# Hybrid encoder block: the low part of q in the sample's scores taken as two 64-row products, one for each half of the keys

## The chip, the cores and the metric

The kernel runs on one core of one Trainium2 chip, so no other core works beside it. The metric is the device time of one execution in microseconds (us), as the median of several runs.

## The reference

The block is computed for a prompt of 512 tokens and for a sample of 1024 tokens, with the same weights. What matters here is the attention: 4 heads, and in each head two score maps m of 64 columns each.

```
s = jnp.einsum('bqhmd,bkhmd->bhmqk', qblk, k,
               preferred_element_type=jnp.float32) * scale
s = s - slopes[None, :, None, None, None] * dist[None, None, None]
p = jax.nn.softmax(s, axis=-1)
w = p[:, :, 0] - lam * p[:, :, 1]
return jnp.einsum('bhqk,bkhd->bqhd', w.astype(v.dtype), v)
```

Ahead of it stand an RMSNorm and one projection (q, k, v and the two inputs of a recurrent branch); behind it the output projection, a residual, and a SwiGLU feed-forward part with its own norm and residual.

## The kernel before

Matrix products run on TensorE in a rounded 32-bit type (F32R). To keep the precision, a factor is split into a high part (the rounded value) and a low part (the rest), and most products are made three times: high by high, high by low, low by high. The helper `mm3` (L213, L214, L215) does that, so these three lines carry most of TensorE's work. Each matrix product is two instructions, a load of the 128x128 weights and a stream of up to 512 columns past them.

The scores have a way of their own. A map has only 64 rows to contract over, and TensorE has 128. So `both` (L493) loads each map's 64 rows of k and q twice, into rows 0 to 63 and again into rows 64 to 127. L504 rounds all 128 rows of k into the tile kt; L505 then puts the low part into rows 64 to 127. One product of 128 rows with the high part of q (tile qh, the same 64 rows twice) thus gives q-high by k-high plus q-high by k-low. A second one, with the low part of q (tile ql), is added to it in PSUM.

For the sample, each head takes 8 blocks of 128 queries (index j), and each block both maps (index m): 4 x 8 x 2 = 64 passes. A pass covers 1024 keys, in two halves of 512 that lie in two banks of PSUM (tile sc, of which there is one). It makes four products of 512 columns, two at L582 and two at L583. VectorE then reads sc with the distance table, writes pb and finds the row minimum (L585), and ScalarE takes the exponential (L588). Transposes (L534) and the products with v (tile pv) follow one block later.

All this is a generator, `attention`, whose steps are put between the steps of other work by `advance`. The sample's attention lies beside the prompt's gate and up projections (tile gu, lines L213 to L215) from about 480 to 850 us. What TensorE does in which order is fixed when the program is built: a scheduler orders the instructions of each engine, and at run time each engine goes through its own list in that order.

The lines ahead of the scores, and the loop that the change touches:

```
A.copy(K[m], r[m])
V.tensor_tensor(K[m][DK:P], r[m][DK:P], K[m][DK:P].bitcast(F32), ALU.subtract)
...
for b in range(n // BLK):
    w = slice(b * BLK, (b + 1) * BLK)
    T.matmul(sc[:, w], lhsT=qh[m][:, qs], rhs=K[m][:, w], start=True, stop=False)
    T.matmul(sc[:, w], lhsT=ql[m][:, qs], rhs=K[m][:, w], start=False, stop=True)
```

`ATT` is the number of buffers in the pool named att, from which kt, v, qh, ql, pb and the transposed weights of a head come.

Of the kernel before, what the change touches and what calls it, by code (L numbers as in the profile page):

```python
# [12 lines left out]
F32R = mybir.dt.float32r  # L13
# [7 lines left out]
P = 128  # L21
# [4 lines left out]
BLK = 512  # L26
NH = 4
DK = 64
# [12 lines left out]
NPAR = 69  # L41

N_RAW, AHEAD, LOOK, LOOK2, LOOK3, LOOK4, LATE = 3, 2, 5, 4, 4, 4, 2
M3, ATT, AL, TH, PG = 10, 15, 2, 4, 16

A1, A2, A3, A4, A5, A6, A7, A8, B1, B2, A9 = 40, 50, 0.05, 80, 180, 12, 290, 0.95, 17, 6, 120
F1, F2, F3, F4, F5, F6 = 0.3, 0.9, 0.3, 0.8, 0.3, 0.5
# [34 lines left out]
def build(tc, io, es):  # L82
    nc = tc.nc
    V, A, T = nc.vector, nc.scalar, nc.tensor
# [16 lines left out]
    def small(n, name, bufs=2):  # L101
        return smp.tile([P, n], F32, name=name, tag=name, bufs=bufs)
# [8 lines left out]
    def bank(name, tag):  # L111
        return banks[tag].tile([P, BLK], F32, name=name, tag=tag)

    def bank2(name, shape):
        return banks["sc"].tile(shape, F32, name=name, tag="sc")
# [24 lines left out]
    def split(h, l, src, eng=V):  # L140
        A.copy(h, src)  # L141
        eng.tensor_tensor(l, src, h.bitcast(F32), ALU.subtract)  # L142
# [68 lines left out]
    def mm3(out, wh, wl, ah, al, first, last, more=False):  # L211

        T.matmul(out, lhsT=wh, rhs=ah, start=first, stop=False, skip_group_check=more)  # L213
        T.matmul(out, lhsT=wh, rhs=al, start=False, stop=False, skip_group_check=more)  # L214
        T.matmul(out, lhsT=wl, rhs=ah, start=False, stop=last, skip_group_check=more)  # L215
# [260 lines left out]
    def two(n, name, dt=F32, ring="att"):  # L476

        if n == BLK:
            t = rings[ring]([P, 2, n], name, dt)
            return [t[:, 0], t[:, 1]]  # L480
        return [rings[ring]([P, n], f"{name}{m}", dt) for m in range(2)]

    def attention(s, done, vo):
        n = length[s]
        nk = n // P
        z = n / SEQ_S
        for hd in range(NH):
            while 8 + hd not in done[s]:
                yield 1.3
            tab = rings["att"]([P, TABW], "tab", F16)  # L490
            nc.sync.dma_start(tab, tabs[hd])

            def both(i, n=n, w=slice(None)):  # L493
                r = two(n, "ld", ring="main")
                for m in range(2):
                    src = qkv[s][i][m * DK:(m + 1) * DK, w]
                    nc.sync.dma_start(r[m][0:DK], src)
                    nc.sync.dma_start(r[m][DK:P], src)
                return r

            r = both(4 + hd)
            K = two(n, "kt", F32R)
            for m in range(2):
                A.copy(K[m], r[m])  # L504
                V.tensor_tensor(K[m][DK:P], r[m][DK:P], K[m][DK:P].bitcast(F32), ALU.subtract)  # L505
                yield 1.2 * z
            vr = rings[vo]([P, n], "vr")
            nc.sync.dma_start(vr, qkv[s][8 + hd])
            vh, vl = two(n, "v", F32R)
            for g in range(n // BLK):  # L510
                w = slice(g * BLK, (g + 1) * BLK)
                pt = bank("pt", "aux")
                for i in range(4):
                    T.transpose(pt[:, i * P:(i + 1) * P], vr[:, g * BLK + i * P:g * BLK + (i + 1) * P], ident)
                split(vh[:, w], vl[:, w], pt)
                yield 0.6
            ot = rings[vo]([P, n], "ot")
            z0 = small(nk, f"z0{nk}")
            ve = small(nk, f"ov{nk}")
            def weights(j, pp, zs):  # L520

                cf = small(1, "cf", 4)
                V.reciprocal(cf, zs[1])
                V.scalar_tensor_tensor(cf, zs[0], neglam, cf, ALU.mult, ALU.mult)
                V.scalar_tensor_tensor(pp[0], pp[1], cf, pp[0], ALU.mult, ALU.add)
                yield 1.5 * z
                if j % 2 == 0:
                    wt.append([[rings["att"]([P, 4, 256], f"wt{x}{i}", F32R) for i in range(nk // 4)] for x in "hl"])
                wh, wl = wt[-1]
                for i in range(nk // 4):  # L530
                    pt = bank("ptw", "aux")
                    for kk in range(4):
                        k0 = (4 * i + kk) * P
                        T.transpose(pt[:, kk * P:(kk + 1) * P], pp[0][:, k0:k0 + P], ident)  # L534
                    jq = slice(j % 2 * P, (j % 2 + 1) * P)
                    split(wh[i][:, :, jq], wl[i][:, :, jq], pt.rearrange("p (k q) -> p k q", k=4))
                    yield 0.7
                if j % 2:
                    yield from values(j // 2, wh, wl)

            def values(g, wh, wl):

                pv = bank("pv", "pv")
                for kc in range(nk):
                    w = slice(kc * P, (kc + 1) * P)
                    mm3(pv[:, 0:256], vh[:, w], vl[:, w], wh[kc // 4][:, kc % 4], wl[kc // 4][:, kc % 4],
                        kc == 0, kc == nk - 1)
                gq = slice(g * 256, (g + 1) * 256)
                A.copy(ot[:, gq], pv[:, 0:256])
                sq = rings["osq"]([P, 256], "osq")  # L550
                A.activation(sq, ot[:, gq], AF.Square)
                yield 2.0 * z

                def squares():
                    for j in range(2):
                        T.matmul(pv[:, 256 + j:257 + j], lhsT=sq[:, j * P:(j + 1) * P], rhs=ones, start=True, stop=True)

                    vg = ve[:, 2 * g:2 * g + 2]
                    zg = z0[:, 2 * g:2 * g + 2]
                    V.scalar_tensor_tensor(vg, zg, EPS, zg, ALU.mult, ALU.mult)  # L560
                    V.scalar_tensor_tensor(vg, pv[:, 256:258], 1.0 / P, vg, ALU.mult, ALU.add)

                late.append(squares)

            wt, late, prev = [], [], None
            for j in range(nk):
                if j % 4 == 0:
                    r = both(hd, BLK, slice(j * P, j * P + BLK))
                    qh, ql = two(BLK, "qh", F32R), two(BLK, "ql", F32R)
                    for m in range(2):  # L570
                        split(qh[m], ql[m], r[m])
                        yield 0.6
                q0 = j * P
                qs = slice(q0 % BLK, q0 % BLK + P)
                pp, zs = two(n, "pb"), []
                if n == BLK:
                    sc2 = bank2("sc2", [P, 2, n])
                for m in range(2):
                    sc = sc2[:, m] if n == BLK else bank2("sc", [P, n])
                    for b in range(n // BLK):  # L580
                        w = slice(b * BLK, (b + 1) * BLK)
                        T.matmul(sc[:, w], lhsT=qh[m][:, qs], rhs=K[m][:, w], start=True, stop=False)  # L582
                        T.matmul(sc[:, w], lhsT=ql[m][:, qs], rhs=K[m][:, w], start=False, stop=True)  # L583
                    mn = small(1, "mn", 4)
                    V.tensor_tensor_reduce(out=pp[m], in0=sc, in1=tab[:, 896 - q0:896 - q0 + n], scale=-0.125,  # L585
                                           scalar=3e38, op0=ALU.add, op1=ALU.min, accum_out=mn)
                    zz = z0[:, j:j + 1] if m == 0 else small(1, "z1", 4)
                    A.activation(pp[m], pp[m], AF.Exp, scale=-1.0, bias=mn, accum_out=zz)  # L588
                    zs.append(zz)
                    if late:  # L590
                        late.pop()()
                    yield 1.5 * z
                    if prev and m == SKEW[0]:
                        yield next(prev)
                    if prev and m == SKEW[1]:
                        yield from prev
                        prev = None
                prev = weights(j, pp, zs)
            yield from prev
            yield YV  # L600
            late.pop()()
            r = rsqrt_cols(ve, nk, "a")
            yield YV * z
            for g in range(n // BLK):
                w = slice(g * BLK, (g + 1) * BLK)
                bc = bcast_cols("pv", r, 4 * g, "a")
                V.scalar_tensor_tensor(ot[:, w], ot[:, w], subg, bc, ALU.mult, ALU.mult)
                nc.scalar.dma_start(cat[s][hd][:, w], ot[:, w])
                yield 1.5
# [217 lines left out]
    n = (B1 + B2 + 3 + GRP) // 2  # L827
# [131 lines left out]
    sc = bank2("sc", [P, 2, BLK])  # L959
# [268 lines left out]
```

## Time and profile before

| | us |
|---|---|
| median of 3 runs | 1773.88 (1773.84 to 1776.88) |
| the profiled execution | 1773.56 |
| its span, first to last instruction | 1771.7 |
| TensorE busy | 1733.3 |
| VectorE busy | 1316.5 |
| ScalarE busy | 829.2 |
| TensorE busy from 480 to 850 us | 367.8 of 370 |

The profiled execution stands 0.32 us below the median of the runs. TensorE's busy time is not TensorE at its peak: products are pipelined, so one is shown as 0.39 us long while the next starts 0.23 us after it. What a product costs is therefore read from the distance of two starts. Loads of weights have rows of their own (PEld) and lie below the product ahead of them.

### The profile page before, as it was taken

How to read it: one execution, taken by the hardware profiler on the slowest of the kernel's cores; microseconds unless marked ns; L12 is line 12 of the kernel's file. 1: busy time of each engine (PE TensorE's matmuls, PEld its weight loads, DVE VectorE, ACT ScalarE, POOL GpSimd, SP SyncE). 2: the span in 40 equal slices, each digit the busy share in tenths (PEclk: the TensorE clock that was granted, in tenths of full speed). 3: DMA queues.
4: the chain of work that ended last, by engine and by line, in shares of the span. 5: the costliest groups of instructions: out<-in, count | busy, mean ns of one | idle time of the engine just before them, and what ended most of it. 6: DMA issues, size and time to landing. Idle time of an engine off the chain costs nothing.

```text
span 1771.7 us, 22720 instructions
## 1 busy us (share of the span) xinstructions
PE 1733.3 (98%) x8316; PEld 1432.2 (81%) x8316; DVE 1316.5 (74%) x2291; ACT 829.2 (47%) x1327; POOL 1.6 (0%) x6
## 2 busy tenths in 40 slices
PE   8999999999999999999999989999999999999997
PEld 7777787777878888888878768888888888888897
DVE  6789878777578777777453797777777777977784
ACT  6568556664355554545242452333233334445451
POOL 0000000000000000000000000000000000000000
PEclk9999999999999999999999999999999999999999
DMA  8533424153373322222364743222233229743261
GB/s 294 193 113 102 152 84 137 60 172 137 115 232 112 105 83 96 77 84 78 125 215 132 258 161 114 89 102 101 98 111 125 89 78 337 256 125 97 95 201 54
DMA packets 105023, 238.77 MB, mean 135 GB/s; under 512 B 12240, under 2 KB 21200, under 8 KB 104912
## 3 DMA queue, kind: packets, MB, share of 16 engines
q1 hardware_dynamic: 76608, 185.04, 32.8%
q10 hardware_dynamic: 28304, 52.28, 7.7%
q8 instruction: 65, 1.06, 0.2%
q14 instruction: 46, 0.38, 0.1%
HBM read 180.00 MB, written 57.28 MB: 134 GB/s over the span
## 4 chain that ended last, share of the span: by engine, by line
PE 84%; DVE 6%; DMA 4%; ACT 3%; issue 1%; SPq 0%; DVEq 0%; ACTq 0%
PE pm L213 5%; PE pm L214 5%; PE pm L215 4%; PE gu L213 4%; PE gu L215 4%; PE gu L214 4%; PE acc L215 4%; PE acc L213 4%; PE acc L214 4%; PE y L213 3%; PE y L214 3%; PE y L215 3%; PE z L214 2%; PE z L213 2%; PE z L215 2%; PE x L213 2%
## 5 line engine op out<-in xcount | busy, mean ns | idle before, releaser
L213 PE MATMUL pm<-xh,wh 128*128 128x512 f32 x480 | 190.5, 397 | 5.6 <-ACT wh L200 3.3
L214 PE MATMUL pm<-xl,wh 128*128 128x512 f32 x480 | 189.7, 395 | 0.8 <-DVE xl L327 0.8
L215 PE MATMUL pm<-xh,wl 128*128 128x512 f32 x480 | 189.4, 395 | 0.0
L200 ACT CAST wh<-wr 128x1024 fp32r<-128x1024 f32 x100 | 104.9, 1049 | 149.9 <-PE gu L214 61.3
L213 PE MATMUL gu<-yh,wh 128*128 128x512 f32 x352 | 142.0, 403 | 0.9 <-DVE ev L375 0.9
L213 PE MATMUL acc<-hp,ws 128*128 128x512 f32 (+1 forms) x396 | 140.9, 356 | 0.0
L215 PE MATMUL acc<-hp,ws 128*128 128x512 f32 (+1 forms) x396 | 140.5, 355 | 0.0
L214 PE MATMUL acc<-hp,ws 128*128 128x512 f32 (+1 forms) x396 | 140.2, 354 | 0.0
L215 PE MATMUL gu<-yh,wl 128*128 128x512 f32 x352 | 139.0, 395 | 0.0
L214 PE MATMUL gu<-yl,wh 128*128 128x512 f32 x352 | 138.7, 394 | 0.0
L201 DVE TENSOR_TENSOR wl<-wr,wh 128x1024 fp32r<-128x1024 f32 x100 | 122.0, 1220 | 17.8 <-ACT wh L200 16.9
L588 ACT ACTIVATE pb<-pb,mn 128x1024 f32<-128x1024 f32 (+1 forms) x96 | 96.9, 1009 | 73.0 <-DVE mn L585 72.9
L585 DVE CUSTOM_DVE_ANT_0 pb<-sc,tab 128x1024 f32<-128x1024 f32 (+1 forms) x96 | 100.0, 1041 | 33.3 <-PE sc L583 31.8
L703 ACT CAST ws<-s 128x512 fp32r<-128x512 f32 x88 | 54.6, 622 | 125.7 <-PE x L215 46.8
L213 PEld LDWEIGHTS pm<-xh,wh 128*128 128x128 f32 x480 | 90.9, 189 | 24.2 <-ACT wh L200 3.5
L214 PEld LDWEIGHTS pm<-xl,wh 128*128 128x128 f32 x480 | 90.8, 189 | 19.6 <-DVE xl L327 1.6
L215 PEld LDWEIGHTS pm<-xh,wl 128*128 128x128 f32 x480 | 90.6, 189 | 19.0 <-DVE wl L201 0.7
L141 ACT CAST hp<-hr 128x512 fp32r<-128x512 f32 (+1 forms) x143 | 77.2, 550 | 54.4 <-PE acc L215 24.6
L142 DVE TENSOR_TENSOR hp<-hr,hp 128x512 fp32r<-128x512 f32 (+1 forms) x143 | 84.6, 603 | 23.7 <-ACT hp L141 20.1
L703 ACT CAST ws<-wr 128x512 fp32r<-128x512 f32 x66 | 41.1, 622 | 100.8 <-PE z L215 43.8
L214 PEld LDWEIGHTS acc<-hp,ws 128*128 128x128 f32 x396 | 75.1, 190 | 10.4
L215 PEld LDWEIGHTS acc<-hp,ws 128*128 128x128 f32 x396 | 75.0, 189 | 10.4
(268 smaller groups left out, 4299.8 us busy)
## 6 DMA issues: line engine op xcount, KB each, us to landing
wr<-w_gate SPq DMA_DIRECT2D x44, 512.0 KB, 3.5
wr<-w_up SPq DMA_DIRECT2D x44, 512.0 KB, 3.5
wr<-w_in SPq DMA_DIRECT2D x40, 512.0 KB, 4.2
hr<-hs SPq DMA_DIRECT2D x77, 256.0 KB, 2.8
hs<-t ACTq DMA_DIRECT2D x44, 256.0 KB, 2.0
hs<-ht ACTq DMA_DIRECT2D x33, 256.0 KB, 2.8
wr<-w_out SPq DMA_DIRECT2D x16, 512.0 KB, 3.5
xd<-xh ACTq DMA_DIRECT2D x28, 256.0 KB, 2.1
```

What stands on the lines that cost most here:

```text
L141: A.copy(h, src)
L142: eng.tensor_tensor(l, src, h.bitcast(F32), ALU.subtract)
L200: A.copy(h, r)
L201: V.tensor_tensor(l, r, h.bitcast(F32), ALU.subtract)
L213: T.matmul(out, lhsT=wh, rhs=ah, start=first, stop=False, skip_group_check=more)
L214: T.matmul(out, lhsT=wh, rhs=al, start=False, stop=False, skip_group_check=more)
L215: T.matmul(out, lhsT=wl, rhs=ah, start=False, stop=last, skip_group_check=more)
L585: V.tensor_tensor_reduce(out=pp[m], in0=sc, in1=tab[:, 896 - q0:896 - q0 + n], scale=-0.125, scalar=3e38, op0=ALU.add, op1=ALU.min, accum_ ...
L588: A.activation(pp[m], pp[m], AF.Exp, scale=-1.0, bias=mn, accum_out=zz)
L703: A.copy(h[:, 0], src)
```

## The change

The products with ql are taken apart from those with qh. For the sample, both qh products come first, as before with 128 rows. Then come two products with 64 rows each: ql's rows 0 to 63 with kt's rows 0 to 63 for keys 0 to 511, at row 0 of the array, and ql's rows 64 to 127 with a new tile ku for keys 512 to 1023, at row 64. They add into the two banks of sc. ku holds, in its rows 64 to 127, the rounded k of the second half of the keys, since kt has the low part there. It is made by one more ScalarE copy of 64x512 for each map of each head (8 in all). The product of q's low part with k's low part, which the 128-row form included, is left out. The pool att gets two more buffers. The prompt's scores keep their form.

```
-M3, ATT, AL, TH, PG = 10, 15, 2, 4, 16
+M3, ATT, AL, TH, PG = 10, 17, 2, 4, 16
...
                 V.tensor_tensor(K[m][DK:P], r[m][DK:P], K[m][DK:P].bitcast(F32), ALU.subtract)
+                if n > BLK:
+
+                    if m == 0:
+                        upper = two(BLK, "ku", F32R)
+                    A.copy(upper[m][DK:P], r[m][DK:P, BLK:])
                 yield 1.2 * z
...
-                    for b in range(n // BLK):
-                        w = slice(b * BLK, (b + 1) * BLK)
+                    blocks = [slice(b * BLK, (b + 1) * BLK) for b in range(n // BLK)]
+                    for w in blocks:
                         T.matmul(sc[:, w], lhsT=qh[m][:, qs], rhs=K[m][:, w], start=True, stop=False)
-                        T.matmul(sc[:, w], lhsT=ql[m][:, qs], rhs=K[m][:, w], start=False, stop=True)
+                        if n == BLK:
+                            T.matmul(sc[:, w], lhsT=ql[m][:, qs], rhs=K[m][:, w], start=False, stop=True)
+                    if n > BLK:
+
+                        T.matmul(sc[:, blocks[0]], lhsT=ql[m][0:DK, qs], rhs=K[m][0:DK, blocks[0]], start=False,
+                                 stop=True, tile_position=(0, 0))
+                        T.matmul(sc[:, blocks[1]], lhsT=ql[m][DK:P, qs], rhs=upper[m][DK:P], start=False,
+                                 stop=True, tile_position=(DK, 0))
```

On TensorE, in the third block of queries of the first head, one pass stands like this before (sc is the score tile, kt and ql as above, gu the prompt's projections):

```order
L213 MATMUL gu<-yh_4419,wh 128x512
L582 MATMUL sc<-kt_4452,qh 128x512
L583 MATMUL sc<-kt_4452,ql 128x512
L582 MATMUL sc<-kt_4452,qh 128x512
L583 MATMUL sc<-kt_4452,ql 128x512
L214 MATMUL gu<-yl_4423,wh 128x512
```

and now like this, where L587 is the old L582, and L592 and L594 are the two products of 64 rows:

```order
L213 MATMUL gu<-yh_4419,wh 128x512
L587 MATMUL sc<-kt_4452,qh 128x512 x2
L592 MATMUL sc<-kt_4452,ql 128x512
L594 MATMUL sc<-ku,ql 128x512
L214 MATMUL gu<-yl_4423,wh 128x512
```

The four instructions are still four, the two of 64 rows stand behind one another, and a product of 128 rows comes before and after them. It is so in 61 of the 64 passes. In the other 3 the products with v (pv) come between the two, as in the third head:

```order
L214 MATMUL pv<-wtl_6289,v_6171 128x256
L215 MATMUL pv<-wth_6287,v_6172 128x256
L594 MATMUL sc<-ku,ql 128x512
L213 MATMUL gu<-yh_4421,wh 128x512
```

There the second product of 64 rows stands alone between products of 128 rows.

On ScalarE, where the first head's k is rounded, the rows were

```order
L504 CAST kt_4452<-ld_4446 128x1024
L504 CAST kt_4453<-ld_4447 128x1024
L141 CAST v_4460<-pt 128x512 x2
```

and are now

```order
L504 CAST kt_4452<-ld_4446 128x1024
L510 CAST ku<-ld_4446 64x512
L504 CAST kt_4453<-ld_4447 128x1024
L510 CAST ku<-ld_4447 64x512
L141 CAST v_4463<-pt 128x512 x2
```

Each map's rounding of k is followed by one copy of 64x512; the second map's rounding stands behind the first map's copy.

## Rows read from the trace of the kernel before

**Rows 1.** Busy time of each engine over the span (the page's first part)
```profile
PE 1733.3 (98%) x8316; PEld 1432.2 (81%) x8316; DVE 1316.5 (74%) x2291; ACT 829.2 (47%) x1327; POOL 1.6 (0%) x6
```
**Rows 2.** The stage of the sample's attention: busy time by engine, clock, DMA
```profile
core 0: us, PE busy (x) PEld busy (x) DVE busy (x) ACT busy (x) POOL busy (x), PEclk, DMA share, GB/s
480.00:850.00 370.00, 367.82 (x1951) 305.05 (x1950) 282.92 (x494) 193.98 (x313) 0.00 (x0) 1.00 0.34 107
```
**Rows 3.** Waits in that stage: TensorE's three (PE), loads before scores (PEld), VectorE's longest
```profile
PE gu L213 <- DVE ev L375: 0.9, 1, 0.9
PE pt L514 <- DMA vr<-qkvs: 0.6, 1, 0.6
PE bc L262 <- DVE dg L261: 0.3, 1, 0.3
...
DVE pb L585 <- PE sc L583: 29.9, 21, 2.4
...
PEld sc L583 <- DVE ql L142: 1.1, 4, 0.3
...
PEld sc L582 <- DVE mn L585: 1.1, 6, 0.2
```
**Rows 4.** Groups by line and shape in that stage: count, busy, mean, idle before
```profile
L585 DVE CUSTOM_DVE_ANT_0 pb<-sc,tab 128x1024 f32<-128x1024 f32 x64 | 78.1, 1220 | 30.9 <-PE sc L583 29.9
...
L582 PE MATMUL sc<-kt,qh 128*128 128x512 f32 x128 | 51.2, 400 | 0.0
L583 PE MATMUL sc<-kt,ql 128*128 128x512 f32 x128 | 50.6, 395 | 0.0
...
L141 ACT CAST qh<-ld 128x512 fp32r<-128x512 f32 x16 | 9.2, 620 | 1.2 <-DVE dg L261 1.2
```
**Rows 5.** Timeline of TensorE's products around one pass: start, length, line, operation
```profile
542.15 0.39 PE L582 MATMUL sc<-kt,qh 128*128 128x512 f32 x1
542.39 0.39 PE L583 MATMUL sc<-kt,ql 128*128 128x512 f32 x1
542.62 0.40 PE L582 MATMUL sc<-kt,qh 128*128 128x512 f32 x1
542.85 0.40 PE L583 MATMUL sc<-kt,ql 128*128 128x512 f32 x1
543.08 0.39 PE L213 MATMUL gu<-yh,wh 128*128 128x512 f32 x1
```
**Rows 6.** Timeline of the weight loads of the same pass
```profile
542.16 0.19 PEld L583 LDWEIGHTS sc<-kt,ql 128*128 128x128 f32 x1
542.39 0.19 PEld L582 LDWEIGHTS sc<-kt,qh 128*128 128x128 f32 x1
542.62 0.19 PEld L583 LDWEIGHTS sc<-kt,ql 128*128 128x128 f32 x1
542.85 0.19 PEld L213 LDWEIGHTS gu<-yh,wh 128*128 128x128 f32 x1
```
**Rows 7.** Timeline of products in the next pass, whose first load came late
```profile
546.05 0.48 PE L582 MATMUL sc<-kt,qh 128*128 128x512 f32 x1
546.37 0.40 PE L583 MATMUL sc<-kt,ql 128*128 128x512 f32 x1
...
547.29 0.39 PE L215 MATMUL gu<-yh,wl 128*128 128x512 f32 x1
547.52 1.03 PE L534 MATMUL ptw<-ident,pb 128*128 128x128 f32 x8
```
**Rows 8.** The late load itself, in the timeline of weight loads
```profile
546.03 0.19 PEld L582 LDWEIGHTS sc<-kt,qh 128*128 128x128 f32 x1 [0.24 <-DVE mn L585]
```

## The prediction

> **What bounds the kernel now.** I read the busy times first. TensorE is busy for 1733.3 us of the span, VectorE for 1316.5 and ScalarE for 829.2 [rows 1], so TensorE is the first suspect everywhere. The change touches one stage, so next I cut that stage out: from 480 to 850 us TensorE is busy for 367.82 of 370 us at the full granted clock (1.00), VectorE for 282.92 and ScalarE for 193.98 [rows 2]. Busy time of pipelined products flatters, so I looked at the waits there: TensorE's products waited 0.9 + 0.6 + 0.3 = 1.8 us in 370, while VectorE waited 29.9 us for scores [rows 3]. The others wait for TensorE. So a microsecond of TensorE's time saved here is a microsecond off the end, and one lost is one on, until VectorE takes over.
>
> **The price of a product.** In an undisturbed pass the four score products start at 542.15, 542.39, 542.62 and 542.85, and the next product at 543.08 [rows 5]: 0.93 us for four, 0.2325 each. That, not the 0.40 us of the groups, is a slot. The stage has 128 products at L582 and 128 at L583 [rows 4], which are 64 passes of four.
>
> **Part 1: two ql products become two of 64 rows in different rows of the array.** The number of columns stays at 512, so each alone still takes a slot; the gain is there only if both stream at the same time. Then a pass takes three slots instead of four. In 61 passes the two stand next to each other; in 3 they are parted by pv products and gain nothing. Removed: 61 x 0.2325 = 14.2 us. No row shows two products at once, so the bounds are 0 (they go one after the other) and 14.2 us (they start together).
>
> **Part 2: the second product's weights.** Every load in the pass begins as the product ahead of its own begins (load 542.16, product 542.15; 542.39 and 542.39; 542.62 and 542.62) [rows 5, 6]: one load ahead, not two. If it stays so, the second product's load begins when the first product begins, and the second starts one load later. What an uncovered load costs shows where one came late: load at 546.03, product at 546.05, next product at 546.37, which is 0.32 us instead of 0.2325 [rows 7, 8]. That is 0.09 us. Bounds: 0, if the load for the other half of the rows goes in early, and 0.09 in each of 61 passes, 5.5 us. I take 5.5, since every load of the rows is one ahead.
>
> **Part 3: going from 128 rows to 64 and back.** It happens twice in a pass and four times in the 3 parted ones: 61 x 2 + 3 x 4 = 134 times. No row of this kernel has a product of fewer than 128 rows, so the cost is open. Lower bound 0: where TensorE goes from the split products to the transposes, another kind of work on the same array, the distance is 547.52 - 547.29 = 0.23 us, a plain slot [rows 7]. Upper bound: the array must empty and the next load can't begin before. Emptying costs what a product's record is longer than its slot, 0.39 - 0.23 = 0.16 us [rows 5]; with the uncovered load it is 0.25 us, 33.5 us in all. I take 0, by the nearest row, and leave the upper end to a rival, because transposes still use all 128 rows and so are not the same case.
>
> **Part 4: the copies and the pool.** Eight ScalarE copies of 64x512 are added. The nearest row, a cast of 128x512, takes 0.62 us [rows 4], so 5.0 us in all on an engine that is idle for 176 us of the stage [rows 2]. The second map's k is rounded 0.62 us later in each head, and VectorE's subtraction behind it too. TensorE never waited for either: before scores its loads waited for ql and for the minimum only, 1.1 us each [rows 3]. I cost it at 0; were it uncovered, it would be 4 heads x 2 x 0.62 = 5.0 us. The two buffers add no instruction; taken as 0.
>
> **Part 5: who is late next.** The sc tile exists once, so the next pass waits until VectorE has read it, 1.22 us [rows 4]. That wait is 1.1 us in the whole stage, in 6 passes [rows 3]. A pass with its other work takes 370 / 64 = 5.8 us and gets 0.14 us shorter, so most of it stays covered; VectorE's share would go from 282.92 of 370 to 282.92 of 361, still 78%. Taken as 0.
>
> **Sum.** -14.2 + 5.5 = -8.7 us. 1773.56 - 8.7 = 1764.9 for the profiled execution, which stands 0.32 us below the median, so 1765.2 by the runs. For this kernel 0.2%, 3.5 us, is about what a measurement can tell from no change.
>
> **Rivals.**
>
> *A. The switch empties the array: slower.* The price is 0.16 us a time, 134 x 0.16 = 21.4 us, so -8.7 + 21.4 = +12.7: 1786.6. If the first load after it is also uncovered, 134 x 0.09 = 12.1 us more: 1798.7. It decides from 8.7 / 134 = 0.065 us a switch. For it: the stage has no slack on TensorE, and no row shows a switch that is free. Against it: going to transposes costs nothing [rows 7]. The Trainium skill (TensorEngine Tiling (Array Packing), Tiling Modes) states this rule outright: changing the tiling mode, as opposed to the tile, drains TensorE. It gives no price, and no run yet shows one; by that rule this rival would be the outcome.
>
> *B. Full overlap: faster.* If the second load goes in early, the pair costs one slot: -14.2, so 1759.7. Against it are the loads that run only one ahead [rows 5, 6]. The Trainium skill (TensorE: Matmul & The Clock Gate, Part 3: Packing small matmuls) says that products in different row groups start about 4 ns apart, and that a load for another row group is pulled ahead; by it the result is this one. The trace of before can't show that.
>
> *C. It does not do what it says.* The two run one after the other, or a small switch price (up to 0.09 us, 12.1 us in all, +3.4) eats the gain: 1773.9 to 1777.3. For it: no row shows two products under way at once. Against it: the two use different rows of the array and different banks of PSUM.
>
> **Chances.** The forecast (one slot saved, one load uncovered, switch nearly free) 0.35, between 1761 and 1770; B 0.10; C 0.15; A 0.40, of which 0.25 lies at up to 1790 and 0.15 above. So faster by over 0.2% is 0.35 + 0.10 = 0.45, within it 0.15, slower 0.40. The likeliest single case is the forecast, 1765. The range starts below B at 1758 and ends at 1790: beyond lies the part of A with uncovered loads, 0.15, and a sliver below.
>
> **What the profile after would show.** Right: the two products of 64 rows start 0.09 us apart, the product after them starts 0.23 us behind the second one, and the stage is some 9 us shorter. B: they start together. A: a gap beyond 0.23 us ahead of the first 64-row product, and one behind the second, with loads that no longer begin at the start of the product ahead. C: starts 0.23 us apart. Part 4 is wrong if TensorE's loads wait for kt or ku, part 5 if the wait for the minimum grows to several us. The prediction as a whole is wrong if a switch costs more than 0.065 us.

## The result and the profile after

The changed kernel takes 1782.72 us (median of 4 runs, 1781.22 to 1784.54) against 1773.86 for the kernel before (median of 4 runs): +8.9 us, a ratio of 1.0052 with a 95% interval of 1.0037 to 1.0067. It is slower; the forecast was 1765, 8.7 us faster. The time lies within the stated range, on the other side of the kernel before.

Busy times by engine, the page's first part, of the changed kernel (before in [rows 1]):

```profile
PE 1740.5 (98%) x8316; PEld 1416.2 (80%) x8316; DVE 1317.7 (74%) x2291; ACT 835.7 (47%) x1335; POOL 1.6 (0%) x6
```

The count of products is the same, 8316. TensorE is busy for 7.2 us more and loads weights for 16.0 us less. This is the stage of the sample's attention, its windows (before in [rows 2]):

```profile
480.00:850.00 370.00, 367.98 (x1900) 283.12 (x1899) 277.26 (x484) 194.02 (x313) 0.00 (x0) 1.00 0.34 107
```

TensorE is as busy as before and at the same clock (1.00), but in the same 370 us it got through 1900 recorded products, not 1951, and VectorE through 484 operations, not 494. The stage got longer; nothing in it got idle. Where, shows in the timeline of TensorE's products around one pass (before in [rows 5]; x2 is two products in one row):

```profile
542.07 0.39 PE L215 MATMUL gu<-yh,wl 128*128 128x512 f32 x1
542.30 0.63 PE L587 MATMUL sc<-kt,qh 128*128 128x512 f32 x2
542.86 0.50 PE L592 MATMUL sc<-kt,ql 64*128 64x512 f32 x1
542.87 0.50 PE L594 MATMUL sc<-ku,ql 64*128 64x512 f32 x1
543.30 0.50 PE L213 MATMUL gu<-yh,wh 128*128 128x512 f32 x1
543.64 0.40 PE L214 MATMUL gu<-yl,wh 128*128 128x512 f32 x1
543.88 0.40 PE L215 MATMUL gu<-yh,wl 128*128 128x512 f32 x1
```

and of the weight loads below it (before in [rows 6]):

```profile
542.08 0.42 PEld L587 LDWEIGHTS sc<-kt,qh 128*128 128x128 f32 x2
542.86 0.18 PEld L592 LDWEIGHTS sc<-kt,ql 64*128 64x128 f32 x1 [0.37 <-issue]
542.86 0.18 PEld L594 LDWEIGHTS sc<-ku,ql 64*128 64x128 f32 x1
543.29 0.19 PEld L213 LDWEIGHTS gu<-yh,wh 128*128 128x128 f32 x1 [0.25 <-issue]
543.40 0.19 PEld L214 LDWEIGHTS gu<-yl,wh 128*128 128x128 f32 x1
543.64 0.19 PEld L215 LDWEIGHTS gu<-yh,wl 128*128 128x128 f32 x1
```

Three things are to be seen. The two 64-row products start 0.01 us apart, and their loads start together: the overlap is complete. Ahead of them the two qh products take 0.56 us for two slots of 0.23, so 0.10 is lost; the pair lasts 0.43, so 0.20 is lost; the product behind it lasts 0.34, so 0.11 is lost. And the loads no longer run one product ahead: the load of the pair begins when the pair does, and so does the load of the next 128-row product (543.29, product at 543.30). "issue" in the brackets means that the load waited for nothing that the profile shows: no semaphore, no other engine. From the first qh product to the second product behind the pair it is 1.34 us; in [rows 5] it would be 0.93 + 0.23 = 1.16. The late load is found at every change in the stage: at all 134 steps between a 128-row and a 64-row product, either way, the load begins 1 to 3 ns ahead of its own product, by the starts in the trace, while for the other products of the stage the median is 223 ns. The pair's first load waits like that 56 times, 19.8 us in all, the longest wait of weight loads in the stage (the view of waits, from 475 to 858 us). This is idle time of the load, about 0.35 us each time, and only part of it is lost to TensorE, which is still streaming the product ahead:

```profile
PEld sc L592 <- issue: 19.8, 56, 0.4
PEld gu L213 <- issue: 9.1, 33, 1.3
```

### The profile page after: what moved, and what is told of

Read it like the earlier page. It is cut to its first block, busy times and chain, and to the rows that moved or that the text cites. A ratio compares the mean times of both kernels' runs of the same rounds, so it can differ in the third digit from the quotient of the medians.

```text
span 1779.1 us, 22728 instructions
## 1 busy us (share of the span) xinstructions
PE 1740.5 (98%) x8316; PEld 1416.2 (80%) x8316; DVE 1317.7 (74%) x2291; ACT 835.7 (47%) x1335; POOL 1.6 (0%) x6
## 4 chain that ended last, share of the span: by engine, by line
PE 86%; DVE 6%; DMA 4%; ACT 3%; issue 1%; SPq 0%; DVEq 0%; ACTq 0%
PE gu L213 5%; PE pm L214 4%; PE pm L213 4%; PE pm L215 4%; PE gu L215 4%; PE gu L214 4%; PE acc L215 4%; PE acc L213 4%; PE acc L214 4%; PE y L213 3%; PE y L215 3%; PE y L214 3%; PE z L214 2%; PE z L215 2%; PE z L213 2%; PE x L215 2%
```

## The experiments

All are edits of the changed kernel. A "change of rows" is a step from a 128-row product to a 64-row one or back, counted in the order of TensorE's instructions; the changed kernel has 134, and 61 of its 64 pairs stand side by side. The theory after the result was that each change costs TensorE some 0.2 us, an emptying of the array and a load that nothing covers, and that the overlap is real and worth a slot. Rival 1 was that the new order, the copies or the larger pool cost the time; rival 2 that 64-row products are slow by themselves.

**e1, everything but the 64 rows.**

```
-T.matmul(sc[:, blocks[0]], lhsT=ql[m][0:DK, qs], rhs=K[m][0:DK, blocks[0]], ..., tile_position=(0, 0))
-T.matmul(sc[:, blocks[1]], lhsT=ql[m][DK:P, qs], rhs=upper[m][DK:P], ..., tile_position=(DK, 0))
+for w in blocks:
+    T.matmul(sc[:, w], lhsT=ql[m][:, qs], rhs=K[m][:, w], start=False, stop=True)
```

Expected: 

> The changed kernel with its order (both qh products, then both ql products), the ku copies and the larger pool, but with ql products of 128 rows as before; ku is made and not read. Theory (each change between 128 rows and 64 rows costs TensorE about 0.20 us, and nothing else in the change costs): no such change is left, so 1774 us, within 0.2% of before. Rival 1 (the order, the copies or the pool cost the time): as the changed kernel, 1782 to 1783. Rival 2 (a product of 64 rows is slow wherever it stands): 1774.

Measured: 1774.29 us, ratio to before 1.0007 (0.9998 to 1.0016). Rival 1 falls: order, copies and pool together cost nothing that can be told (2.8 us at the end of the interval). In the stage its trace has TensorE's products in the same order as the changed kernel's, 1836 of them, so the two can be laid beside each other product by product.

**e7, one 64-row product a pass.**

```
+T.matmul(sc[:, blocks[1]], lhsT=ql[m][:, qs], rhs=K[m][:, blocks[1]], start=False, stop=True)
 T.matmul(sc[:, blocks[0]], lhsT=ql[m][0:DK, qs], rhs=K[m][0:DK, blocks[0]], ..., tile_position=(0, 0))
-T.matmul(sc[:, blocks[1]], lhsT=ql[m][DK:P, qs], rhs=upper[m][DK:P], ..., tile_position=(DK, 0))
```

Expected: 

> One 64-row product a pass (keys 0 to 511, at row 0), behind a ql product of 128 rows for keys 512 to 1023: no overlap, 128 changes of rows. Theory: 128 x 0.20 = +25.6 us, 1799. Rival 2 (the 64-row product itself takes 0.43 in place of 0.23, with no price of the change): 64 x 0.20 = +12.8, 1787. Rival 1: 1782 to 1783.

Measured: 1795.68 us, ratio 1.0123 (1.0110 to 1.0136): +22.0 us over 128 changes, 0.17 each, and 3.6 us less than the theory's 25.6. Its timeline takes the price apart, since every product has a row of its own:

```profile
503.91 0.39 PE L592 MATMUL sc<-kt,ql 128*128 128x512 f32 x1
504.23 0.50 PE L593 MATMUL sc<-kt,ql 64*128 64x512 f32 x1
504.66 0.50 PE L213 MATMUL gu<-yh,wh 128*128 128x512 f32 x1
504.99 0.39 PE L214 MATMUL gu<-yl,wh 128*128 128x512 f32 x1
505.22 0.39 PE L215 MATMUL gu<-yh,wl 128*128 128x512 f32 x1
```

With a slot of 0.23, the 128-row product ahead keeps TensorE 0.09 too long (504.23 - 503.91 = 0.32), the 64-row product 0.20 (0.43), the one behind 0.10 (0.33). The records of the two that start with an uncovered load are 0.50 long instead of 0.39: 0.11. So the 0.20 in the middle is that load, 0.11, and 0.09 of emptying; the 0.10 behind is the second load. One change is 0.09 and 0.11. The starts alone give the same split, since 0.09 stands by itself ahead of the 64-row product and 0.10 by itself behind it. That the 0.09 is the array emptying is a reading: the rows show that neither a load nor a product starts in it.

**e4, four changes a pass.** Each 64-row product behind the qh product of its half.

```
 for w in blocks:
     T.matmul(sc[:, w], lhsT=qh[m][:, qs], rhs=K[m][:, w], start=True, stop=False)
     if n == BLK:
         ...
+    elif w is blocks[0]:
+        T.matmul(sc[:, w], lhsT=ql[m][0:DK, qs], rhs=K[m][0:DK, w], ..., tile_position=(0, 0))
+    else:
+        T.matmul(sc[:, w], lhsT=ql[m][DK:P, qs], rhs=upper[m][DK:P], ..., tile_position=(DK, 0))
```

Expected: 

> Each 64-row product right behind the qh product of its half of the keys: no overlap, 256 changes of rows. Theory: 256 x 0.20 = +51 us over before, 1825. Rival 2 (128 products, each 0.20 us slower than a slot): +26 us, 1800. Rival 1: 1783.

Measured: 1820.17 us, ratio 1.0262 (1.0245 to 1.0279): +46.4 over 256 changes, 0.18 each, some 5 us less than the theory's 51. The qh product between two 64-row ones pays as they do, in the timeline:

```profile
504.75 0.39 PE L587 MATMUL sc<-kt,qh 128*128 128x512 f32 x1
505.07 0.50 PE L591 MATMUL sc<-kt,ql 64*128 64x512 f32 x1
505.50 0.49 PE L587 MATMUL sc<-kt,qh 128*128 128x512 f32 x1
505.92 0.49 PE L594 MATMUL sc<-ku,ql 64*128 64x512 f32 x1
506.34 0.50 PE L213 MATMUL gu<-yh,wh 128*128 128x512 f32 x1
506.69 0.40 PE L214 MATMUL gu<-yl,wh 128*128 128x512 f32 x1
```

The second qh product, with all 128 rows, lasts 0.42 (505.50 to 505.92). It is not the 64 rows that are slow, but every step between the two kinds.

**e2, no overlap.** Both products at row 0 of the array.

```
-T.matmul(sc[:, blocks[0]], lhsT=ql[m][0:DK, qs], rhs=K[m][0:DK, blocks[0]], ..., tile_position=(0, 0))
-T.matmul(sc[:, blocks[1]], lhsT=ql[m][DK:P, qs], rhs=upper[m][DK:P], ..., tile_position=(DK, 0))
+for w in blocks:
+    T.matmul(sc[:, w], lhsT=ql[m][0:DK, qs], rhs=K[m][0:DK, w], ..., tile_position=(0, 0))
```

Expected: 

> Both 64-row products use rows 0 to 63 of the array, so they can't stream at once; the changes of rows stay as in the changed kernel. Theory: the slot comes back, 61 x 0.23 = 14.2 us above the changed kernel: 1797. Rival 2 (each 64-row product 0.43): 61 x 0.43 = 26 us above it: 1809. If the overlap had been worth nothing: 1783.

Measured: 1797.39 us, ratio 1.0133 (1.0116 to 1.0149), 14.7 us above the changed kernel: the saved slot, as worked out (14.2), within the some 4 us that the two intervals leave. It had 134 changes too, and 23.6 / 134 = 0.18. In the timeline of a pass the two products take 0.66 us (503.20 to 503.86), where the pair took 0.43:

```profile
502.65 0.61 PE L587 MATMUL sc<-kt,qh 128*128 128x512 f32 x2
503.20 0.73 PE L593 MATMUL sc<-kt,ql 64*128 64x512 f32 x2
503.86 0.50 PE L213 MATMUL gu<-yh,wh 128*128 128x512 f32 x1
```

**e3, the pair twice.**

```
+T.matmul(sc[:, blocks[0]], lhsT=ql[m][0:DK, qs], ..., stop=False, tile_position=(0, 0))
+T.matmul(sc[:, blocks[1]], lhsT=ql[m][DK:P, qs], ..., stop=False, tile_position=(DK, 0))
 T.matmul(sc[:, blocks[0]], lhsT=ql[m][0:DK, qs], ..., stop=True, tile_position=(0, 0))
 T.matmul(sc[:, blocks[1]], lhsT=ql[m][DK:P, qs], ..., stop=True, tile_position=(DK, 0))
```

Expected: 

> The pair is made twice in a row, so the low part of q counts twice in the sample's scores; 132 changes of rows, nearly as in the changed kernel (134). Theory: a pair between 64-row products costs one slot, 62 x 0.23 = 14.4 us above the changed kernel: 1797. Rival 2 (a pair takes 0.43 wherever it stands): 64 x 0.43 = 27.5 above it: 1810.

Measured: 1798.44 us, ratio 1.0141 (1.0126 to 1.0157), 15.7 us above the changed kernel, or 0.25 a pass. The timeline of a pass:

```profile
504.91 0.62 PE L587 MATMUL sc<-kt,qh 128*128 128x512 f32 x2
505.46 0.50 PE L592 MATMUL sc<-kt,ql 64*128 64x512 f32 x1
505.46 0.50 PE L594 MATMUL sc<-ku,ql 64*128 64x512 f32 x1
505.80 0.39 PE L596 MATMUL sc<-kt,ql 64*128 64x512 f32 x1
505.81 0.39 PE L598 MATMUL sc<-ku,ql 64*128 64x512 f32 x1
506.12 0.50 PE L215 MATMUL gu<-yh,wl 128*128 128x512 f32 x1
```

The second pair's records are 0.39 long, as of a product whose load was covered. It starts 0.34 behind the first, which is a slot and the first pair's load, and lasts 0.32, a slot and the emptying. Between pairs nothing is lost. Rival 2, which wanted 27.5, falls here and in e4 and e7.

**e5, one map of two.** Map 0 with the pair, map 1 as before (70 changes, 29 pairs side by side).

```
-if n == BLK:
+if n == BLK or m == 1:
...
-if n > BLK:
+if n > BLK and m == 0:
```

Expected: 

> The 64-row pair for map 0 only; map 1 is as before; all copies and the pool stay. 70 changes of rows in place of 134, 29 pairs side by side in place of 61. Theory: 70 x 0.20 - 29 x 0.23 = +7.3 us at most, and half of the measured +8.9 at least, so 1778 to 1781. Rival 1 (copies or pool): 1782 to 1783. Rival 2: 1778.

Measured: 1780.82 us, ratio 1.0033 (1.0021 to 1.0045): +7.1 by the medians, at the upper end of what was expected, and more than half of the changed kernel's +8.9. With 29 slots saved (6.7 us) that is 0.20 a change; the interval of the ratio, 3.7 to 8.0 us, allows 0.15 to 0.21, so this run can't tell 0.20 from the 0.17 of the changed kernel.

**e6, no product with the low part of q.**

```
-T.matmul(sc[:, w], lhsT=qh[m][:, qs], rhs=K[m][:, w], start=True, stop=False)
+T.matmul(sc[:, w], lhsT=qh[m][:, qs], rhs=K[m][:, w], start=True, stop=n > BLK)
...
-T.matmul(sc[:, blocks[0]], lhsT=ql[m][0:DK, qs], rhs=K[m][0:DK, blocks[0]], ..., tile_position=(0, 0))
-T.matmul(sc[:, blocks[1]], lhsT=ql[m][DK:P, qs], rhs=upper[m][DK:P], ..., tile_position=(DK, 0))
```

Expected: 

> Leaves out the products with the low part of q in the sample's scores altogether, so two slots a pass instead of four. If the stage is bound by TensorE all through, 128 x 0.2325 = 29.8 us less: 1744. If VectorE or the single score tile takes over, less comes out: 1750 to 1760. It tells how far a microsecond of TensorE is a microsecond of the end.

Measured: 1744.37 us, ratio 0.9833 (0.9818 to 0.9847): -29.3 us of the 29.8 taken from TensorE. A slot gained or lost in this stage is one at the end.

**e9 and e8, half the changes.** If the price goes with the changes, two pairs for each pair of changes should come out even. For that, both maps' scores must lie in PSUM at once: one tile of four banks. e9 has that layout with 128-row products, e8 with the pairs of both maps behind one another. This is e8; e9 has two ql products of 128 rows in place of the last two lines.

```
+four = bank2("sc", [P, 2, n])
+scs = [four[:, 0], four[:, 1]]
+for m in range(2):
+    for w in blocks:
+        T.matmul(scs[m][:, w], lhsT=qh[m][:, qs], rhs=K[m][:, w], start=True, stop=False)
+for m in range(2):
+    T.matmul(scs[m][:, blocks[0]], lhsT=ql[m][0:DK, qs], ..., tile_position=(0, 0))
+    T.matmul(scs[m][:, blocks[1]], lhsT=ql[m][DK:P, qs], ..., tile_position=(DK, 0))
...
-psum(ps, mm=3, sc=1, pv=1, aux=2)
+psum(ps, mm=2, sc=1, pv=1, aux=1)
```

Expected of e9: 

> The control of e8: both maps' scores of a block in one tile of four banks of PSUM, so eight products stand together, and all ql products have 128 rows. In the attention stage the prompt's projections get 2 banks instead of 3 and the transposes 1 instead of 2; after it the banks are as before. No 64-row product. The price of the lost banks is unknown: 0 to +30 us over before, 1774 to 1804.

Expected of e8: 

> As e9, but the ql products are 64-row pairs, both maps' pairs behind one another: 84 changes of rows in place of 134, about 60 pairs side by side. With the price that the runs so far give, 0.175 us a change (46.4 us over 256 changes is 0.18, 21.9 over 128 is 0.17): 84 x 0.175 - 60 x 0.2325 = +0.7 us over e9, between -2 and +3. If the price went with the pairs and not with the changes, +9 over e9, as the changed kernel over before.

Measured: e9 1773.34 us, ratio to before 1.0002 (0.9992 to 1.0013); e8 1777.56, ratio 1.0014 (1.0002 to 1.0026). The new layout as a whole costs nothing that can be told. By the medians e8 is 4.2 us over e9 where +0.7 was expected, just outside what was named; by the two ratios it is 2.1 us, inside, and their intervals leave almost 3 us either way. Part of it is a count: 56 of its pairs stand side by side, not 60, so 13.0 us are saved. That makes (4.2 + 13.0) / 84 = 0.20 a change by the medians and 0.18 by the ratios. The +9 of a price that goes with the pairs is not there.

**e11 and e10, still fewer changes.** As e9 and e8, with the eight score products put ahead of other ready work when TensorE's order is made.

```
+with tc.high_priority():
+    for m in range(2):
+        ...
```

Expected of e11: 

> The control of e10: e9 (both maps' scores in one tile of four banks, all products of 128 rows) with the eight score products put ahead of other ready work in the order of TensorE, so that they stand together. e9 took 1773.3. Expected 1771 to 1776.

Expected of e10: 

> As e11, with the 64-row pairs of both maps: 70 changes of rows in place of e8's 84, and all 64 pairs side by side. Theory with 0.175 us a change: 70 x 0.175 - 64 x 0.2325 = -2.6 us against e11, so 1769 to 1773, the point where the pair pays; with 0.20 a change, -0.9. If the price went with the pairs, +4 or more against e11, as e8 against e9 (+4.2).

Measured: e11 1773.74 us, ratio 1.0008 (0.9999 to 1.0017); e10 1772.87, ratio 0.9996 (0.9987 to 1.0006). With 70 changes for 64 pairs the whole loss is gone: -0.9 us against e11 by the medians, -2.1 by the ratios, with more than 2 us either way. That fits 0.20 a change (-0.9) as well as 0.175 (-2.6), and not +4 or more. The timeline of one block in e10 (x4 is the four qh products):

```profile
505.61 1.07 PE L590 MATMUL sc<-kt,qh 128*128 128x512 f32 x4
506.60 0.49 PE L592 MATMUL sc<-kt,ql 64*128 64x512 f32 x1
506.61 0.49 PE L594 MATMUL sc<-ku,ql 64*128 64x512 f32 x1
506.94 0.39 PE L592 MATMUL sc<-kt,ql 64*128 64x512 f32 x1
506.94 0.39 PE L594 MATMUL sc<-ku,ql 64*128 64x512 f32 x1
507.26 0.50 PE L215 MATMUL gu<-yh,wl 128*128 128x512 f32 x1
507.60 0.39 PE L213 MATMUL gu<-yh,wh 128*128 128x512 f32 x1
```

From the first qh product to 507.60 it is 1.99 us, where eight products of 128 rows and the one behind them take 8 x 0.2325 + 0.23 = 2.09. This is the shortest such block: the nine blocks in the trace that two products of 512 columns follow have a median of 2.03, and the same nine products take 2.07 in e11. e10 is not a version that beats the kernel before: its interval takes in 1. It shows the point where the pair pays.

## Why the prediction was wrong

**What bounds the stage.** Right. TensorE sets it, and e6 gave back 29.3 of 29.8 us.

**Part 1, a slot saved in 61 passes, 14.2 us.** Right: e2, without the overlap, is 14.7 us slower than the changed kernel, and the starts of the second products, laid beside those of e1, give 14.3 us.

**Part 2, the second load uncovered, 5.5 us.** Wrong: 0. I took it that loads run one product ahead, from loads that all fill the same 128 rows. The loads of the two halves start together (542.86 both), and the products 0.01 us apart. What is uncovered is the load of the whole pair, at the step from 128 to 64 rows, and that belongs to part 3. Here rival B was right, and so was the Trainium skill (TensorE: Matmul & The Clock Gate, Part 3: Packing small matmuls) with its start some 4 ns apart.

**Part 3, the step between 128 and 64 rows at 0.** This is the step that failed. I took the lower bound "by the nearest row", the step from the split products to the transposes, which is free [rows 7], although the text itself said that it is not the same case: both sides of that step use all 128 rows. The rows of e7 give 0.09 of emptying and 0.11 of uncovered load for each change, 0.20. By the totals it is 0.17 (changed kernel, (8.9 + 14.2) / 134), 0.17 (e7) and 0.18 (e2, e4); e5, e8 and e10 give 0.18 to 0.20 and can't tell these apart. With 134 changes at 0.17 it is 23 us against 14.2 saved.

The totals stand below the rows for a reason that the traces show. Laid beside e1, with its same order, the products at the 134 steps of the changed kernel take 25.5 us more, 0.19 a step; the 61 second products of the pairs give back 14.3; and all other products of the stage take 2.7 us less: 25.5 - 14.3 - 2.7 = +8.5 us in these two traces. Counted so, a step costs 0.19 in e2 and e7 (beside e1) and in e4 (beside the kernel before) as well. Part of the 2.7 is loads that waited for another engine and now mostly come in time, such as those of the products at L561, which take 6.1 us in all in e1 and 5.8 in the changed kernel. The waits of their loads, in e1 and then in the changed kernel (475 to 858 us), are:

```profile
PEld pv L561 <- ACT osq L556: 3.6, 9, 0.4
PEld pv L561 <- ACT osq L556: 1.2, 3, 0.4
```

Both parts of the price stood in the upper bound, the load at the right size (0.09 to 0.11) and the emptying at 0.16, nearly twice what it is: the 0.39 of a record minus its slot is more than what a step loses to emptying.

**Rival A** was the outcome. It decided from 0.065 us a change, or from 14.2 / 134 = 0.106 once the second load costs nothing, and the measured price of 0.19 is well above either. It gave 1786.6 because it had 0.16 for emptying alone and paid 5.5 for the second load; the measured 1782.7 is made of other terms, and that the two lie so near is in part luck. Its variant with uncovered loads, 1798.7, had both terms of the price but each step too dear. The Trainium skill (TensorEngine Tiling (Array Packing), Tiling Modes) said it outright: a change of the tiling mode, not of the tile, drains TensorE. The trace agrees as far as it goes, with 0.09 us at each step in which nothing starts, and e3 shows the other half of the sentence, a pair behind a pair that loses nothing. It had spoken against the change before the run, and the one row held against it was of another kind.

**Part 4, copies and pool at 0.** Right: e1. The eight copies took 5.0 us on ScalarE, and the view of their line names nothing that waited for them:

```profile
L510 ACT CAST ku<-ld x8: 617/620/621, 492.1 to 764.7; 64x512 fp32r<-64x512 f32 x8
```

The reading behind it was not complete: the loads before scores waited not only for ql and for the minimum, but also for work of ScalarE, to which the copies were added. The kernel before has this line, which [rows 3] leave out:

```profile
PEld sc L582 <- ACT wth L141: 0.8, 3, 0.3
```

**Part 5, VectorE not late.** It was not put to the test, since the stage got longer. In e6, with two slots fewer a pass, VectorE still did not take over. The loads' wait for the minimum, 1.1 us in [rows 3], is no longer in the changed kernel's view of waits.

**What stays open.** The 0.09 is called emptying because nothing starts in it; no run separates that from another cause of the delay. Which loads account for the rest of the 2.7 us was not followed up. All the steps here are between products of 128 and 64 rows with 512 columns and 128 columns of weights; no run shows another size.

## What to carry to other kernels

Before small products are packed into part of TensorE's rows, count the steps between full and part rows in the order that TensorE gets: here each cost about 0.19 us, so a lone pair of 512 columns, which saves 0.23, loses on a trip there and back of 0.38, and two pairs for one trip come out about even. A bound of zero must come from a row that has the thing whose price is sought (here, fewer than 128 rows); where no row has it, the choice between far ends is open, and a written rule that names the case weighs more than a row that only looks like it.

## What was not expected of the hardware

Loads for the two halves of the rows run at the same time, 0.18 us each from the same start (542.86), while loads of 128 rows start behind one another: one product apart as a rule, and 0.11 us apart where the first is late (543.29 and 543.40). And two of the eight banks of PSUM that the stage's pools hold could be moved from the projections and the transposes to the score tile (e9) at a ratio of 1.0002. No run shows whether the two banks hid nothing where they were or whether the larger score tile gave back what they had hidden.
